# Second layer's down projection of a two-layer decoder by Strassen's scheme of seven products

## The chip, the cores and the metric

The kernel runs on one core of one Trainium2 chip. The metric is the device time of one execution in microseconds, as the median over runs; lower is better. A core has a TensorE (PE in the profile, with PEld for its weight loads), a VectorE (DVE), a ScalarE (ACT), a GpSimd (POOL) and a SyncE (SP). Each engine takes its own instructions in their order. SP, ACT and POOL also issue DMA transfers between the chip's memory and the on-chip memory SBUF.

## The reference

The model is a two-layer decoder over 512 tokens of width 1024, in float32. Each layer ends with a feed-forward block whose hidden width is 2816, and only the second layer's block is touched here:

```python
def conv_ffn(x, ln_g, up_w, conv_w, conv_b, down_w):
    u = causal_dwconv(rms_norm(x, ln_g) @ up_w, conv_w, conv_b)
    gate, up = u[..., :FFN_DIM], u[..., FFN_DIM:]
    return (jax.nn.silu(gate) * up) @ down_w
...
        ff = conv_ffn(x, ffn_ln_g[layer], ffn_up_w[layer], ffn_conv_w[layer],
                      ffn_conv_b[layer], ffn_down_w[layer])
        x = x + ff.astype(x.dtype)
```

The down projection is thus a product of a 512 x 2816 matrix (the hidden values) with a 2816 x 1024 matrix (the weights), and its result is added to the residual stream.

## The kernel before

Every float32 product is made of three products of rounded parts: each operand is split into a high part (a copy to the fp32r type, made by ACT) and a low part (the difference, made by DVE), and PE adds high x high, high x low and low x high into PSUM. One such matrix instruction multiplies a 128 x 128 block into 512 columns.

Weights come as chunks of 128 x 1024 values (512 KB). The list `plan` names them in order of use. `emit_chunk` takes the next one: a DMA issued by SP brings it into one of three raw buffers (`wr_...`), ACT makes `wh_...`, DVE makes `wl_...`, both in rings of three buffers. `chunk(key)` hands out the chunk and sees to it that two more are begun (`AHEAD = 2`).

The second layer's feed-forward (`ffn` with `nnext` None) goes through the 2816 hidden columns in 22 blocks of 128, in two parts of 12 and 10. In the up projection `products` makes, for each block, 24 matrix instructions for the gate (`ps_g`) and 24 for the up side (`ps_u`). `taps` scales a PSUM tile by the row norm on DVE (`uu`, `ug`, L953), applies the three convolution taps (one on ACT, two on DVE, L956), and after SiLU on ACT the block is the product of both sides (L1023). Its high part `hh` is made by ACT (L1024), its low part `hl` by DVE (L1025).

After each part `down_tokens` makes the down projection with hidden values as the stationary operand: for each of two halves of 512 output columns it goes through the part's blocks, and for each block through four blocks of 128 tokens, three matrix instructions each (L992 to L994). The sums are added to `xr`, which holds the residual stream by tokens. In the last part the result is stored in pieces of 128 x 256 by ACT and SP, and the very last products are made in two halves of 256 columns (`end`, L986 to L988) so that the first half's addition and store start earlier.

A scheduler in the kernel's framework turns the program into one queue for each engine; within a queue, an instruction that waits holds up those behind it.

## Time and profile before

| | |
|---|---|
| Median of 3 runs | 1345.41 us (1345.1 to 1346.06) |
| Profiled execution | 1346.14 us |
| ... its span on the chip | 1344.4 us |
| HBM read, written | 131.64 MB, 2.25 MB |
| First down projection of the second layer begins | 1112.3 us after the span's start |
| Second one begins | 1286.4 us |

A page of the profile gives each engine's busy time, the chain of waits that ended last, and groups of instructions as line, engine, operation and "tile written <- tiles read", with the shapes, the count, busy microseconds and the mean in nanoseconds, then the engine's idle time before them and what ended it. A timeline's row begins with the start and the duration in microseconds. PE's matrix instructions are pipelined: each row's duration is longer than the step from one start to the next.

### The profile page before, as it was taken

Reading aid. Unit: us, or ns where it says so; the run is one execution under the profiler, and the core shown is the slowest. Engines: PE = TensorE matmul, PEld = TensorE weight load, DVE = VectorE, ACT = ScalarE, POOL = GpSimd, SP = SyncE. Lnnn points to the kernel's source line nnn. Section 1 sums busy time; section 2 is a strip of 40 time slices with the busy share of each in tenths; the row PEclk is TensorE's granted clock in tenths of the full one; section 3 lists DMA queues with packets and bytes.
Section 4 is the critical chain, followed back from the end, with each engine's and each line's share of the span. In section 5 each row is a group of like instructions: output and inputs, shape, how many; then the busy total and the mean of one; then the engine's idle time right before and its main releaser. Section 6 shows DMA issues by size and latency. Waiting matters only on the chain.

```text
span 1344.4 us, 17006 instructions
## 1 busy us (share of the span) xinstructions
PE 1339.6 (100%) x6468; PEld 1101.9 (82%) x6468; DVE 925.9 (69%) x1554; ACT 645.5 (48%) x1067; POOL 97.8 (7%) x139
## 2 busy tenths in 40 slices
PE   9999999999999999999999999999999999999998
PEld 8878888888888888888888887777888888888887
DVE  7989888889877774367755556778777773367743
ACT  6696554653444442134433556777654442134420
POOL 4230301200110000000002200000100000000000
PEclk9999999999999999999999999999999999999999
DMA  7553533432333333333323423221233333333332
GB/s 205 153 157 95 149 95 114 129 95 70 95 94 98 103 97 94 95 95 101 95 80 111 125 79 94 71 79 49 63 94 94 95 94 94 96 106 96 95 94 79
DMA packets 179826, 135.00 MB, mean 100 GB/s; under 512 B 6492, under 2 KB 163552, under 8 KB 179744
## 3 DMA queue, kind: packets, MB, share of 16 engines
q1 hardware_dynamic: 173872, 120.73, 30.4%
q0 software_dynamic: 4592, 12.08, 3.0%
q8 instruction: 51, 0.84, 0.3%
q10 hardware_dynamic: 1280, 1.10, 0.2%
q14 instruction: 31, 0.25, 0.1%
HBM read 131.64 MB, written 2.25 MB: 100 GB/s over the span
## 4 chain that ended last, share of the span: by engine, by line
PE 98%; DVE 1%; ACT 1%; issue 0%
PE ps_g L205 6%; PE ps_u L206 6%; PE ps_u L204 6%; PE ps_g L206 6%; PE ps_g L204 6%; PE ps_u L205 6%; PE ps_in L204 5%; PE ps_in L206 5%; PE ps_in L205 5%; PE ps_d L206 3%; PE ps_d L205 3%; PE ps_d L204 3%; PE ps_d L992 3%; PE ps_d L994 3%; PE ps_d L993 3%; PE ps_o L205 2%
## 5 line engine op out<-in xcount | busy, mean ns | idle before, releaser
L204 PE MATMUL ps_u<-xgh,wh_u 128*128 128x512 f32 x352 | 137.4, 390 | 0.0
L205 PE MATMUL ps_g<-xgl,wh_g 128*128 128x512 f32 x352 | 137.1, 389 | 0.0
L204 PE MATMUL ps_g<-xgh,wh_g 128*128 128x512 f32 x352 | 137.0, 389 | 0.0
L206 PE MATMUL ps_u<-xgh,wl_u 128*128 128x512 f32 x352 | 137.0, 389 | 0.0
L206 PE MATMUL ps_g<-xgh,wl_g 128*128 128x512 f32 x352 | 137.0, 389 | 0.0
L205 PE MATMUL ps_u<-xgl,wh_u 128*128 128x512 f32 x352 | 136.9, 389 | 0.0
L204 PE MATMUL ps_in<-xgh,wh_in 128*128 128x512 f32 x304 | 122.9, 404 | 0.0
L158 DVE TENSOR_TENSOR wl_d<-wr_d,wh_d 128x1024 fp32r<-128x1024 f32 (+1 forms) x46 | 54.2, 1178 | 96.9 <-ACT wh_d L147 96.7
L206 PE MATMUL ps_in<-xgh,wl_in 128*128 128x512 f32 x304 | 119.7, 394 | 0.0
L205 PE MATMUL ps_in<-xgl,wh_in 128*128 128x512 f32 x304 | 119.1, 392 | 0.0
L147 ACT ACTIVATE wh_d<-wr_d 128x1024 fp32r<-128x1024 f32 (+1 forms) x46 | 47.1, 1024 | 130.6 <-PE ps_d L994 62.4
L953 DVE TENSOR_TENSOR uu<-ps_u,nr_f 128x512 f32<-128x512 f32 x44 | 30.4, 691 | 77.6 <-PE ps_u L206 77.6
L1024 ACT ACTIVATE hh<-vg 128x512 fp32r<-128x512 f32 x44 | 27.8, 632 | 114.9 <-DVE vg L1023 114.9
L205 PEld LDWEIGHTS ps_g<-xgl,wh_g 128*128 128x128 f32 x352 | 66.1, 188 | 14.0 <-DVE xgl L484 0.3
L206 PEld LDWEIGHTS ps_u<-xgh,wl_u 128*128 128x128 f32 x352 | 66.1, 188 | 13.8
L204 PEld LDWEIGHTS ps_g<-xgh,wh_g 128*128 128x128 f32 x352 | 66.1, 188 | 13.7
L206 PEld LDWEIGHTS ps_g<-xgh,wl_g 128*128 128x128 f32 x352 | 66.0, 188 | 13.7
L205 PEld LDWEIGHTS ps_u<-xgl,wh_u 128*128 128x128 f32 x352 | 66.1, 188 | 13.6
L204 PEld LDWEIGHTS ps_u<-xgh,wh_u 128*128 128x128 f32 x352 | 66.1, 188 | 13.5
L147 ACT ACTIVATE wh_g<-wr_g 128x1024 fp32r<-128x1024 f32 x44 | 46.7, 1061 | 50.5 <-PE ps_u L205 31.1
L204 PE MATMUL ps_d<-hh,wh_d 128*128 128x512 f32 x176 | 68.5, 389 | 0.0
L205 PE MATMUL ps_d<-hl,wh_d 128*128 128x512 f32 x176 | 68.5, 389 | 0.0
(374 smaller groups left out, 3198.9 us busy)
## 6 DMA issues: line engine op xcount, KB each, us to landing
wr_g<-in_ffn_up_w_dram SPq DMA_DIRECT2D x44, 512.0 KB, 3.8
wr_u<-in_ffn_up_w_dram SPq DMA_DIRECT2D x44, 512.0 KB, 3.9
wr_d<-in_ffn_down_w_dram SPq DMA_DIRECT2D x42, 512.0 KB, 3.7
wr_in<-in_ssm_in_w_dram SPq DMA_DIRECT2D x40, 512.0 KB, 3.9
m<-cumd POOLq DMA_DIRECT2D x16, 512.0 KB, 4.5
wr_out<-in_ssm_out_w_dram SPq DMA_DIRECT2D x16, 512.0 KB, 3.5
wr_k<-in_kv_w_dram SPq DMA_DIRECT2D x8, 512.0 KB, 3.8
wr_q<-in_q_w_dram SPq DMA_DIRECT2D x8, 512.0 KB, 4.0
```

Of the source, the lines that this page charges most:

```text
L147: return act.activation(self.wh[:, :self.n], self.raw[:, :self.n], AF.Copy)
L158: return eng.tensor_tensor(out=self.wl[:, :self.n], in0=self.raw[:, :self.n], in1=self.wh[:, :self.n].bitcast(F32), op=ALU.subtract)
L204: pe.matmul(ps, wh, xh, start=start, stop=False)
L205: pe.matmul(ps, wh, xl, start=False, stop=False)
L206: return pe.matmul(ps, wl, xh, start=False, stop=stop).ins
L953: dve.tensor_tensor(out=u, in0=ps, in1=r, op=ALU.mult)
L992: pe.matmul(pss[b], hh[k][:, ts], wh[:, k - k0, :], start=k == 0, stop=False)
L993: pe.matmul(pss[b], hh[k][:, ts], wl[:, k - k0, :], start=False, stop=False)
L994: pe.matmul(pss[b], hl[k][:, ts], wh[:, k - k0, :], start=False, stop=k == stop)
L1024: act.activation(h, ga, AF.Copy)
```

## The change

The hidden values are cut in two by tokens (first and last 256) and in two by blocks (even and odd), the weights in two by blocks and in two by output columns. Of the eight block products of a 2 x 2 product the scheme makes seven, of sums of blocks, and adds them up. With A the hidden values (first index token half, second index even or odd blocks) and B the weights (even or odd blocks, column half), the operands are:

| Product | Hidden values | Weights |
|---|---|---|
| 1 | A11 | B11 |
| 2 | A12 | B21 |
| 5 | S1 = A21 - A22 | B11 + B12 |
| 7 | A11 - A21 | B12 + B22 |
| 6 | S2 = S1 - A11 | B11 + B12 + B22 |
| 3 | A12 + S2 | B22 |
| 4 | A22 | B11 + B12 + B22 + B21 |

The blocks are now taken in three parts of 8, 8 and 6, so of 4, 4 and 3 pairs. DVE makes the four sums of hidden values for each pair, and ACT and DVE the high and low parts of seven operands (`operands`). A part's weights B11, B12 and B22 are loaded by SP during its up projection (`ahead`) into the tiles z, x and y; z is two new tiles, x and y lie in `xT`, which is free by then. Ahead of each of these loads POOL copies one column from a hidden block into the tile. B21 alone still comes through the raw buffers. The weights of 5, 6 and 4 are made in z: when a product's weights have been split, POOL issues a DMA that adds the next quarter into z (`plus`). Those of 7 are a sum on DVE. A chunk now covers one product and one or two pairs: 12 or 6 matrix instructions. The products run in the order 1, 2, 5, 7, 6, 3, 4, and within a chunk those with low weights come last. A running sum on DVE (`run_sum`) shares partial results.

```diff
+PARTS_D = (0, 8), (8, 16), (16, 22)
+SEVEN = "1257634"
...
             if l == 1:
-
-                for c in range(2):
-                    for k in range(p0, p1, 2):
-                        plan.append(("d%d_%d_%d" % (l, c, k), *w_cols(ffn_down_w[l], k, 2, c * 512, 512)))
+                for m in SEVEN:
+                    for q0 in range(0, (p1 - p0) // 2, 2):
+                        plan.append(("s%s_%d_%d" % (m, p0, q0), (m, p0, q0, min(2, (p1 - p0) // 2 - q0))))
...
+            def plus(t, p0, q0, nq, j, i):
+                pool.dma_start(view(t, nq), source(p0, q0, nq, j, i), accum_op=ALU.add)
+
+            def ahead(p0, n, behind):
+
+                for k, j, i in ("z", 0, 0), ("x", 0, 1), ("y", 1, 1):
+                    for q0 in range(0, n // 2, 2):
+                        c, nq = q0 // 2, min(2, n // 2 - q0)
+                        pool.tensor_copy(raws[k][c][:, 0:1], behind[:, 0:1])
+                        sync.dma_start(view(raws[k][c], nq), source(p0, q0, nq, j, i))
+
+            def combine(key, m, p0, q0, nq):
+
+                c, n = q0 // 2, nq * 512
+                if m == "2":
+                    t = wrp.tile([P, 1024], F32, tag="raw", name="wr_" + key)
+                    sync.dma_start(view(t, nq), source(p0, q0, nq, 1, 0))
+                else:
+                    t = raws["x" if m == "7" else "y" if m == "3" else "z"][c]
+                    if m == "7":
+                        dve.tensor_tensor(out=t[:, :n], in0=t[:, :n], in1=raws["y"][c][:, :n], op=ALU.add)
...
+                act.activation(wh[:, :n], t[:, :n], AF.Copy)
+                dve.tensor_tensor(out=wl[:, :n], in0=t[:, :n], in1=wh[:, :n].bitcast(F32), op=ALU.subtract)
+                ready.append((key, view(wh, nq), view(wl, nq)))
+                if m in "156":
+                    plus(t, p0, q0, nq, *{"1": (0, 1), "5": (1, 1), "6": (1, 0)}[m])
...
+                    s = fp.tile([P, 4, 256], F32, tag="sums", name="sums%d" % p, bufs=1)
+                    for o, a, b, op in ((0, e[:, 1], h[:, 1], ALU.subtract), (1, s[:, 0], e[:, 0], ALU.subtract),
+                                        (2, e[:, 0], e[:, 1], ALU.subtract), (3, h[:, 0], s[:, 1], ALU.add)):
+                        dve.tensor_tensor(out=s[:, o], in0=a, in1=b, op=op)
+                    parts = [(slice(3, 7), s), (slice(1, 3), h)]
+                for o, v in parts:
+                    act.activation(sh[:, o], v, AF.Copy)
+                    dve.tensor_tensor(out=sl[:, o], in0=v, in1=sh[:, o].bitcast(F32), op=ALU.subtract)
...
+                    for low in range(2):
+                        for b in bs:
+                            for q in qs:
+                                h, w = (t[:, side[m], b * P:(b + 1) * P] for t in sides[q][:2])
+                                if low:
+                                    pe.matmul(pss[b], h, ws[q][1][:, cols], start=False, stop=end and q == qs[-1])
+                                    continue
+                                pe.matmul(pss[b], h, ws[q][0][:, cols], start=first and q == qs[0], stop=False)
+                                pe.matmul(pss[b], w, ws[q][0][:, cols], start=False, stop=False)
...
+                        elif m == "6":
+                            add(r, pss[b])
+                            add(to(b, 512), r, ALU.subtract)
+                            add(r, seven[b])
+                            add(to(2 + b, 512), r, ALU.subtract)
+                            add(to(2 + b, 0), r)
```

The orders of the queues up to the second layer's first block are the same as before. At three places they show what moved.

SP, before, in the up projection of the second layer around blocks 5 and 6 (`wr_g1_5` is the raw buffer for block 5's gate weights):

```order
L139 DMA wr_g1_5_8982<-in_ffn_up_w_dram 128x8x128
L139 DMA wr_u1_5_9020<-in_ffn_up_w_dram 128x8x128
L139 DMA wr_g1_6_9062<-in_ffn_up_w_dram 128x8x128
L139 DMA wr_u1_6_9100<-in_ffn_up_w_dram 128x8x128
L139 DMA wr_g1_7_9142<-in_ffn_up_w_dram 128x8x128
```

and the same place now (`wz0`, `wz1` are z, `xT` is x and y):

```order
L140 DMA wr_g1_5_9007<-in_ffn_up_w_dram 128x8x128
L140 DMA wr_u1_5_9045<-in_ffn_up_w_dram 128x8x128
L994 DMA wz0_8586<-in_ffn_down_w_dram 128x2x512
L994 DMA wz1_8587<-in_ffn_down_w_dram 128x2x512
L994 DMA xT_85<-in_ffn_down_w_dram 128x2x512 x4
L140 DMA wr_g1_6_9087<-in_ffn_up_w_dram 128x8x128
```

The first part's six loads of down weights now stand between block 5's and block 6's up weights.

DVE, before, from the last block's up side (`uu1_21`) into the second down projection (`wl_d1_0_16` is the low part of a chunk of down weights):

```order
L953 TENSOR_TENSOR uu1_21_10787<-ps_u1_21_10762,nr_f1_8671 128x512
L158 TENSOR_TENSOR wl_d1_0_16_10805<-wr_d1_0_16_10802,wh_d1_0_16_10804 128x1024
L956 SCALAR_TENSOR_TENSOR vu1_21_10788<-uu1_21_10787,cf1_105,vu1_21_10788 128x511
L956 SCALAR_TENSOR_TENSOR vu1_21_10788<-uu1_21_10787,cf1_105,vu1_21_10788 128x510
L1023 TENSOR_TENSOR vg1_21_10750<-vg1_21_10750,vu1_21_10788 128x512
L1025 TENSOR_TENSOR hl1_21_10794<-vg1_21_10750,hh1_21_10793 128x512
L158 TENSOR_TENSOR wl_d1_0_18_10835<-wr_d1_0_18_10832,wh_d1_0_18_10834 128x1024
```

and now (`wl_s2_16_0` is the low part of product 2's weights for the first two pairs of the part that begins at block 16, `wl_s2_16_2` that of its third pair, `ps_s1_16_0` the sum of product 1 for the first 128 tokens, `sl20` the low operands of the pair 20, 21):

```order
L957 TENSOR_TENSOR uu1_21_11046<-ps_u1_21_11021,nr_f1_8674 128x512
L1009 TENSOR_TENSOR wl_s2_16_0_11067<-wr_s2_16_0_11064,wh_s2_16_0_11066 128x1024
L960 SCALAR_TENSOR_TENSOR vu1_21_11047<-uu1_21_11046,cf1_105,vu1_21_11047 128x511
L1009 TENSOR_TENSOR wl_s2_16_2_11085<-wr_s2_16_2_11082,wh_s2_16_2_11084 128x512
L960 SCALAR_TENSOR_TENSOR vu1_21_11047<-uu1_21_11046,cf1_105,vu1_21_11047 128x510
L1059 TENSOR_TENSOR xr_8585<-xr_8585,ps_s1_16_0_11062 128x512
L1132 TENSOR_TENSOR vg1_21_11010<-vg1_21_11010,vu1_21_11047 128x512
L1059 TENSOR_TENSOR xr_8585<-xr_8585,ps_s1_16_1_11063 128x512
L1035 TENSOR_TENSOR sums21_11053<-vg1_20_10931,vg1_21_11010 128x256
L1039 TENSOR_TENSOR sl20_10976<-vg1_21_11010,sh20_10975 128x512
L1035 TENSOR_TENSOR sums21_11053<-sums21_11053,vg1_20_10931 128x256
L1009 TENSOR_TENSOR wl_s5_16_0_11101<-wz0_8586,wh_s5_16_0_11100 128x1024
```

The split of product 2's second chunk and the additions for product 1 now stand ahead of the last pair's low operands.

DVE, now, around product 6 of the last part:

```order
L1009 TENSOR_TENSOR wl_s6_16_0_11171<-wz0_8586,wh_s6_16_0_11170 128x1024
L1009 TENSOR_TENSOR wl_s6_16_2_11188<-wz1_8587,wh_s6_16_2_11187 128x512
L1009 TENSOR_TENSOR wl_s3_16_0_11201<-xT_85,wh_s3_16_0_11200 128x1024
L1009 TENSOR_TENSOR wl_s3_16_2_11217<-xT_85,wh_s3_16_2_11216 128x512
L1059 TENSOR_TENSOR run_sum_8588<-run_sum_8588,ps_s6_16_0_11198 128x512
L1059 TENSOR_TENSOR run_sum_8588<-run_sum_8588,ps_s6_16_1_11199 128x512
L1059 TENSOR_TENSOR xr_8585<-xr_8585,run_sum_8588 128x512 x2
L1059 TENSOR_TENSOR run_sum_8588<-run_sum_8588,ps_s7_16_0_11168 128x512
L1059 TENSOR_TENSOR run_sum_8588<-run_sum_8588,ps_s7_16_1_11169 128x512
L1059 TENSOR_TENSOR xr_8585<-xr_8585,run_sum_8588 128x512 x4
L1009 TENSOR_TENSOR wl_s4_16_0_11243<-wz0_8586,wh_s4_16_0_11242 128x1024
```

Ten additions stand between product 3's and product 4's weights.

131 lines of the change are left out of this document (91 added, 40 removed).

## The prediction

> **What bounds the kernel now.** I read the page's engine shares first, then its chain of waits, then the stages of the second layer's feed-forward, then single instructions.
>
> ```profile
> span 1344.4 us, 17006 instructions
> PE 1339.6 (100%) x6468; PEld 1101.9 (82%) x6468; DVE 925.9 (69%) x1554; ACT 645.5 (48%) x1067; POOL 97.8 (7%) x139
> PE 98%; DVE 1%; ACT 1%; issue 0%
> ```
>
> TensorE is busy for the whole span and makes up 98% of the chain: no wait is left to remove, and only fewer products, or cheaper ones, shorten it. The view of busy time by stage, cut at the first down projection, the up projection of blocks 12 to 21, the second down projection and the tail, says how much room the other engines have:
>
> ```profile
> 1112.30:1177.60 65.30, 65.30 (x289) 54.06 (x289) 22.67 (x24) 14.07 (x14) 0.00 (x0) 1.00 0.32 96
> 1177.60:1286.40 108.80, 108.80 (x481) 90.09 (x480) 76.82 (x96) 47.76 (x59) 0.00 (x0) 1.00 0.33 98
> 1286.40:1341.00 54.60, 54.60 (x247) 45.30 (x245) 19.47 (x29) 9.82 (x10) 0.00 (x0) 1.00 0.25 78
> ```
>
> Columns: length, then busy us of PE, PEld, DVE, ACT and POOL, granted clock, DMA share, GB/s. PE fills each stage; DVE is at 71% in the up projection (76.82 of 108.80) and at 35% in the down projections. The price of a product is its pitch, not the 0.39 us of its row, since products overlap:
>
> ```profile
> 1135.46 0.39 PE L992 MATMUL ps_d<-wh_d,hh 128*128 128x512 f32 x1
> 1135.68 0.39 PE L993 MATMUL ps_d<-wl_d,hh 128*128 128x512 f32 x1
> L992 PE MATMUL ps_d<-wh_d,hh 128*128 128x512 f32 x174 | 67.7, 389 | 0.0
> L986 PE MATMUL end<-wh_d,hh x4: 278/283/283, 1339.5 to 1340.5; 128*128 128x256 f32 x4
> 1339.81 0.28 PE L986 MATMUL end<-wh_d,hh 128*128 128x256 f32 x1
> 1340.77 0.28 PE L988 MATMUL end<-wh_d,hl 128*128 128x256 f32 x1
> ```
>
> The first down projection has 288 products of 512 columns in 65.30 us: 0.2267 us each (1135.46 to 1135.68 shows one step). The eight steps from 1339.81 to 1340.77 give 0.12 us for one of 256 columns.
>
> **The products removed (term 1).** Before: 2 column halves x 22 blocks x 4 token blocks x 3 = 528, of which the last 6 are cut into 12 half-width ones: 522 full (three lines of 174) and 12 half. After: 7 sums x 11 pairs x 2 token blocks x 3 = 462, the last 3 cut into 6: 459 full and 6 half. Saved: 63 x 0.2267 + 6 x 0.12 = 15.0 us. The new order inside a product (low weights last) loads one stationary tile per product as before, so it changes no pitch.
>
> **DVE's new work (term 2).** These rows price it:
>
> ```profile
> L158 DVE TENSOR_TENSOR wl_d<-wr_d,wh_d 128x1024 fp32r<-128x1024 f32 x42 | 51.5, 1226 | 96.9 <-ACT wh_d L147 96.7
> L1025 DVE TENSOR_TENSOR hl<-vg,hh 128x512 fp32r<-128x512 f32 x11 | 7.6, 693 | 7.7 <-ACT hh L1024 7.7
> 1140.83 1.23 DVE L158 TENSOR_TENSOR wl_d<-wr_d,wh_d 128x1024 fp32r<-128x1024 f32 x1 [4.21 <-ACT wh_d L147]
> 1141.97 1.28 DVE L999 TENSOR_TENSOR xr<-ps_d,xr 128x512 f32<-128x512 f32 x2
> 1283.19 1.53 DVE L956 SCALAR_TENSOR_TENSOR vg<-ug,cf,vg 128x511 f32<-128x511 f32 x2
> 1336.94 0.76 DVE L1005 TENSOR_TENSOR xr<-ps_d,xr 128x256 f32<-128x256 f32 x2 [0.67 <-PE ps_d L994]
> 1341.09 0.42 DVE L1005 TENSOR_TENSOR xr<-end,xr 128x256 f32<-128x256 f32 x1 [0.29 <-PE end L988]
> L147 ACT ACTIVATE wh_d<-wr_d 128x1024 fp32r<-128x1024 f32 x42 | 44.6, 1062 | 124.8 <-PE ps_d L994 62.4 <-PE ps_d L205 49.2 <-PE ps_u L205 6.6
> ```
>
> Queued back to back, independent DVE instructions overlap by some 0.08 us: the split that starts at 1140.83 is followed at 1141.97, so 1.14 us for 1024 columns; the pair of 0.69 takes 1.28, so 0.60 for 512; the pair of 0.42 takes 0.76, so 0.34 for 256. The two taps (L956) take 1.53.
>
> In the up projection two blocks take PE 4 x 24 x 0.2267 = 21.8 us and DVE now 71% of that, 15.4. Two low parts of 512 go (1.2); four sums of 256, and low parts of 256, 512 and 1024 come (3.4), and per part two sums of 1024 for product 7 (0.6 per two blocks): 18.2 us, 84%. Still under PE; cost nothing.
>
> In the down projection of a part of eight blocks PE has 168 x 0.2267 = 38.1 us. DVE has: the rest of the last block (PSUM times norm 0.60, taps 1.53, gate times up 0.60, three sums 1.0, low parts 0.60 and 1.14: 5.5), twelve splits (13.7), 22 additions (13.2; ten of them after product 6), two splits for the next blocks (2.3): 34.7. It fits, but with one thin place. Product 2's second chunk needs the second half of the last block's operands after 36 products, 8.2 us. Ahead of them DVE has, counting in queue order, 0.60, 0.3 of waiting for ACT's copy, 1.14, 1.53, the second split of product 2 (it stands before the gate product) 1.14, 0.60, 0.60, 0.34, 0.60, 0.34, and then 0.69: 7.9 us. Margin 0.3; I take 0.
>
> In the last part PE has 123 x 0.2267 + 6 x 0.12 = 28.6 us, and DVE 5.5, six splits of 1024 and six of 512 (10.4), 22 additions (13.2) and two of 256 (0.7): 29.8 us. So there DVE ends last. It also waits some 1.4 us: 0.3 at the start, 0.3 for product 3's buffer, 0.5 for the end of product 6, the rest in handoffs. It ends about 31.3 us after the last up product, 2.7 past PE. Before, DVE's last addition ended at 1341.51, 55.1 us after 1286.4, where PE needed 234 x 0.2267 + 12 x 0.12 = 54.5: 0.6 past. Cost: 2.1 us. If DVE were slower or its queue less full of ready work, this is the term that grows; if PE were held up elsewhere, it shrinks.
>
> **The accumulating loads (term 3).** After product 1's weights are split, z takes another quarter of the matrix by a DMA from POOL that adds into SBUF, and so after 5 and 6. No row shows such a transfer. The nearest:
>
> ```profile
> wr_d<-in_ffn_down_w_dram SPq DMA_DIRECT2D x42, 512.0 KB, 3.7
> m<-cumd POOLq DMA_DIRECT2D x16, 512.0 KB, 4.5
> wr_d<-in_ffn_down_w_dram SPq DMA_DIRECT2D x4, 256.0 KB, 3.1
> DMA to landing us min/median/max: 3.8/4.5/7.9
> out_dram<-xr SPq DMA_DIRECT2D x8, 128.0 KB, 1.9
> out_dram<-xr ACTq DMA_DIRECT2D x8, 128.0 KB, 2.6
> ```
>
> The half-size load is 0.6 us shorter, so 512 KB move in about 1.2 us. From below: 4.5, as POOL's plain load of this size (the fourth line is its spread). From above: three times that, 13.5. Reading the target too doubles the moving part only: 4.5 + 1.2 = 5.7, which I take as nearest to the row. Its deadline: the split of the sum before must end, the load land, and ACT copy 1.06 us before PE starts the next use. In the last part product 5's split ends at 8.5 us (0.1 of handoff, 0.60, 0.3 of waiting, 1.14, 0.75, 0.60, 0.75, 0.60, 0.60, 0.60, 0.34, 0.60, 0.34, 1.23 in queue order), product 6 starts at 72 x 0.2267 = 16.3: 6.7 us for the load. Ten more rows and its own (0.34, 0.60, 0.60, 1.14, 0.60, 1.14, 0.60, 2.40, 1.23) bring product 6's split to 17.1; product 4 starts at 108 x 0.2267 = 24.5: 6.3 us. In the parts of eight blocks these are 11 us or more, 9.7 once the first load itself delays the second split. So 5.7 is covered, by 0.6 at the worst place. With a spread that reaches 7.9 I add 0.5 us. What is late otherwise: ACT's copy for product 6 waits, behind it on ACT the copies for product 3, and PE for both; two such waits per part. On POOL only other accumulations stand behind.
>
> **What is moved (term 4).** Six loads of a part (3 MB) stand on SP between two up-weight loads, for the first part behind block 5's. POOL's six one-column copies ahead of them have by then long been done (block 2). A load on SP has this slack:
>
> ```profile
> 1228.90 0.37 SPq L139 DMA_DIRECT2D wr_g<-in_ffn_up_w_dram  x1
> 1231.99 1.06 ACT L147 ACTIVATE wh_g<-wr_g 128x1024 fp32r<-128x1024 f32 x1 [0.94 <-PE ps_u L205]
> 1237.43 1.07 ACT L147 ACTIVATE wh_u<-wr_u 128x1024 fp32r<-128x1024 f32 x1 [0.28 <-PE ps_g L205]
> 1242.87 1.06 ACT L147 ACTIVATE wh_g<-wr_g 128x1024 fp32r<-128x1024 f32 x1 [0.94 <-PE ps_u L205]
> ```
>
> With three raw buffers the load issued at 1228.90 is the one split at 1242.87, 14.0 us later, and PE reads it two chunks of 24 products (10.9 us) later, since the plan runs two chunks ahead. The next load is issued one chunk (5.4 us) after, behind six of 1.2 us; even if all seven ran one after another at 3.7 (25.9 us), it would land 24 us after its issue and cost PE under 2. I take 0. On ACT two stores of the last part stand ahead of product 6's copy and wait for product 2's additions at 12 us; that copy is not due before 15. The very last store moves from SP to ACT: by the two rows above 0 to 0.7 us; I take 0.3.
>
> **Sum.** -15.0 + 2.1 + 0.5 + 0.3 = -12.1 us. The profiled execution took 1346.14 with a span of 1344.4: 1334.0, with a span of 1332.3. The median of the runs shown is 0.7 lower: 1345.41 - 12.1 = 1333.3 us.
>
> **The rivals.** A: the accumulating load takes twice the plain one, 9.0 us. Both deadlines of the last part are missed, by 2.3 and 2.7, less the 0.5 allowed: 1333.3 + 4.5 = 1337.8. For it: an add must read both operands; against it: only a third of the 4.5 scales with size. (The Trainium skill, Collectives: The Full Stack, section "The bandwidth ceiling", says that a transfer with an add ran at about half the rate of a copy, 32.35 against 62.28 GB/s, because it reads two sources. By that rule on the whole 4.5 us this rival holds, on the moving part alone the 5.7 above; no run shows it yet.)
>
> B: DVE instructions on one accumulator don't overlap, since each addition to the output tile or to the running sum touches what the one before wrote. Then about 40 instructions in the last part cost 0.08 more, 3.2, and the thin places in the two earlier parts (margin 0.3 against ten such steps, and the ten additions ahead of product 4's split) some 1.9 each: 1333.3 + 7.0 = 1340.3. For it: dependent taps take 1.53, no overlap; against it: most neighbours in the new queue are independent.
>
> C, slower: the accumulating loads are far slower than any load here. Each microsecond of their time A costs 2 past 6.5 us in the last part and 4 more past 9.7 in the other two: -12.6 + 2(A - 6.5) + 4(A - 9.7) is zero at A = 10.7. At 13.5, three times the row, it is +16.6: 1362.0. Against it: the longest POOL load of this size took 7.9.
>
> D: nothing but the products counts, because loads and DVE stay hidden: 1345.4 - 15.0 = 1330.4. Against it the 29.8 to 28.6 above.
>
> **Chances.** The forecast 0.46, A 0.18, B 0.13, C 0.13, D 0.05; 0.05 is left for the meeting of A and C near zero and for what I don't see. The forecast alone lies within 1331 to 1335; the range takes in A, B and D: 1330 to 1342. A change under 0.2% (2.7 us) can't be told from none. Faster: the forecast, A, B and D, 0.82; slower: C and 0.02 of the rest, 0.15; same 0.03.
>
> **What would show it.** Step 1: three lines of products that total 459 + 6 at a pitch of 0.2267. Step 2: DVE busy over 90% from the last up product to the end, PE idle about 2 us there and under 0.5 at the two earlier parts. Step 3: the adding loads land within 6.3 us and ACT's copies for products 6 and 4 wait for them without PE waiting. Step 4: no wait of PE in the up projection. The prediction is wrong if PE idles before product 6 or 4 behind those copies, or before product 2's second chunk behind DVE.

## The result and the profile after

| | Before | After |
|---|---|---|
| Median of 4 runs each, same chip | 1345.31 us (1345.1 to 1346.06) | 1333.62 us (1333.47 to 1334.21) |
| Ratio, 95% interval | | 0.9913 (0.9896 to 0.993) |
| Profiled execution, its span | 1346.14, 1344.4 us | 1333.75, 1332.1 us |

The change made the kernel 11.7 us faster; 1333.3 was predicted, in a range of 1330 to 1342. The page of the kernel after:

```profile
PE 1325.3 (99%) x6399; PEld 1088.0 (82%) x6399; DVE 1001.3 (75%) x1678; ACT 671.6 (50%) x1104; POOL 121.8 (9%) x175
PE 94%; DVE 4%; ACT 1%; DMA 1%; issue 0%; SPq 0%; POOL 0%; DVEq 0%; ACTq 0%
```

TensorE lost 14.3 us of busy time (1339.6 to 1325.3) and the span lost 12.3. The chain, 98% TensorE before, now runs 4% through VectorE. How the stages share this, the view of busy time by stage says (length; busy us of PE, PEld, DVE, ACT and POOL; granted clock; DMA share; GB/s). The stages are the down projection of the first part, the up and down projection of the second, and the down projection of the third:

```profile
1067.83:1105.91 38.08, 38.08 (x170) 31.53 (x168) 33.20 (x43) 18.69 (x20) 4.83 (x4) 1.00 0.51 96
1105.91:1192.95 87.04, 87.04 (x386) 72.07 (x384) 70.81 (x96) 38.27 (x50) 3.56 (x8) 1.00 0.48 140
1192.95:1231.03 38.08, 38.08 (x170) 31.53 (x168) 33.18 (x43) 18.68 (x20) 4.83 (x4) 1.00 0.50 95
...
1296.31:1326.72 30.41, 30.24 (x130) 23.34 (x128) 28.01 (x42) 13.60 (x18) 4.19 (x4) 1.00 0.48 96
```

The parts of eight blocks take 38.08 us each, which is 168 products at 0.2267 us and nothing else; the up projection of eight takes 87.04, which is 384 products. So in these stages TensorE waits nowhere up to 1296.31, where the last part begins. That part would take 28.6 us at the same pitch and takes 30.41, with VectorE busy for 28.01 of it (92%), and 5.38 us pass behind it.

For a comparison that does without the run's beginning, take the first product of the second layer's feed-forward, before and after. The timeline of the kernel before:

```profile
977.08 0.39 PE L204 MATMUL ps_g<-xgh,wh_g 128*128 128x512 f32 x1
```

and of the kernel after:

```profile
976.09 0.39 PE L208 MATMUL ps_g<-xgh,wh_g 128*128 128x512 f32 x1
```

The work ahead of it is the same, so the 0.99 us is between two executions and not the change's (in the other kernels below, whose work up to here is the same too, it stands between 976.29 and 977.53). From there to the end of the span: 367.32 us before, 356.01 after, 11.31 less. (The medians say 11.7.)

How VectorE comes into the last part and ends it, in its timeline after (start, duration, instruction, in brackets the idle time ahead of it and what ended it):

```profile
1279.41 1.23 DVE L1005 TENSOR_TENSOR xT<-xT 128x1024 f32<-128x1024 f32 x1 [1.91 <-DMA xT<-in_ffn_down_w_dram]
...
1296.51 0.69 DVE L957 TENSOR_TENSOR uu<-ps_u,nr_f 128x512 f32<-128x512 f32 x1 [0.17 <-PE ps_u L210]
1298.05 1.23 DVE L1009 TENSOR_TENSOR wl_s<-wr_s,wh_s 128x1024 fp32r<-128x1024 f32 x1 [0.85 <-ACT wh_s L1008]
...
1304.19 1.22 DVE L1009 TENSOR_TENSOR wl_s<-wz,wh_s 128x1024 fp32r<-128x1024 f32 x1
...
1313.49 1.23 DVE L1009 TENSOR_TENSOR wl_s<-wz,wh_s 128x1024 fp32r<-128x1024 f32 x1 [0.60 <-ACT wh_s L1008]
1315.25 0.69 DVE L1009 TENSOR_TENSOR wl_s<-wz,wh_s 128x512 fp32r<-128x512 f32 x1 [0.53 <-ACT wh_s L1008]
1316.20 1.83 DVE L1009 TENSOR_TENSOR wl_s<-xT,wh_s 128x1024 fp32r<-128x1024 f32 x2 [0.25 <-ACT wh_s L1008]
...
1321.54 2.49 DVE L1059 TENSOR_TENSOR xr<-xr,run_sum 128x512 f32<-128x512 f32 x4
1323.94 1.82 DVE L1009 TENSOR_TENSOR wl_s<-wz,wh_s 128x1024 fp32r<-128x1024 f32 x2
1325.68 2.47 DVE L1059 TENSOR_TENSOR xr<-xr,ps_s 128x512 f32<-128x512 f32 x4
1328.26 0.75 DVE L1059 TENSOR_TENSOR xr<-xr,end 128x256 f32<-128x256 f32 x2
```

VectorE ends at 1329.01, 32.70 us after the last up product. It waited 2.4 us there (the five brackets from 1296.51 on) and 0.1 at the end, so 30.2 us are work. From 1316.20 on its queue has no gap of note: TensorE's last products, those with product 4's low weights, wait for the splits at 1323.94, and the four additions from 1325.68 are still running when they are done. Behind VectorE's end 3.09 us of storing follow (before: 1344.4 - 1341.51 = 2.89).

The first row stands in the up projection ahead of that part: VectorE waits 1.91 us for x and y, which it adds up for product 7, and no room is left behind it to make that up (one gap of 0.29 us until 1296.51). The chain that ended last passes through this load, and from there through VectorE's queue to TensorE's wait at 1303.99:

```profile
1270.98 8.31 DMA xT<-in_ffn_down_w_dram
```

How much of the wait reaches the last part, other kernels' executions say, whose queue on VectorE in this up projection is the same. In the kernels below called "four additions later", "no adding loads" and "six additions left out" it was 1.12, 1.48 and 1.75 us, and VectorE began product 2's first split (here at 1298.05) 1.06, 1.31 and 1.57 us after the last up product; here, with 1.91, 1.74. So a wait of 1.12 us is absorbed (1.06 is also the start in parts of six that VectorE enters with time to spare), and here 0.7 us come through.

The bookkeeping from the first up product on: products 15.0 less; VectorE's end 32.70 - 28.6 = 4.1 us past what TensorE needs, where it was 0.6 before, 3.5 more; storing 0.2 more: -11.3.

The loads that add into z, on the page (512 KB each, median us to landing):

```profile
wz<-in_ffn_down_w_dram POOLq DMA_DIRECT2D x15, 512.0 KB, 6.0
```

and in the view of their line (POOL's time for an issue in ns, min/median/max; then who waited, us and times):

```profile
L986 POOL DMA_DIRECT2D wz<-in_ffn_down_w_dram x18: 889/1190/1517, 1060.2 to 1316.2; - x18
  ACT wh_s L1008: 15.2, 6
```

They take 6.0 us, and ACT's copies of z waited for them six times, 15.2 us in all. The last part's, in the timeline of POOL and ACT (a row of POOL's holds two loads, issued one after the other; those for product 4 start at 1315.02):

```profile
1305.94 2.12 POOL L986 DMA_DIRECT2D wz<-in_ffn_down_w_dram  x2 [10.23 <-DVE sums L1035]
...
1312.40 1.06 ACT L1008 ACTIVATE wh_s<-wz 128x1024 fp32r<-128x1024 f32 x1 [4.55 <-DMA wz<-in_ffn_down_w_dram]
1314.58 0.63 ACT L1008 ACTIVATE wh_s<-wz 128x512 fp32r<-128x512 f32 x1 [1.12 <-DMA wz<-in_ffn_down_w_dram]
...
1320.89 1.06 ACT L1008 ACTIVATE wh_s<-wz 128x1024 fp32r<-128x1024 f32 x1 [4.21 <-DMA wz<-in_ffn_down_w_dram]
```

The first load of product 6 is issued at 1305.94 and copied from 1312.40, 6.5 us later; the second, behind it on POOL, only from 1314.58. TensorE's timeline shows a little of that, and one wait for VectorE ahead of it (a row's start is set against the start of the row ahead plus 0.2267 us for each of its products):

```profile
1303.12 0.73 PE L1055 MATMUL ps_s<-wh_s,sh 128*128 128x512 f32 x2
1303.99 0.74 PE L1056 MATMUL ps_s<-wh_s,sl 128*128 128x512 f32 x2
...
1312.87 0.61 PE L1053 MATMUL ps_s<-wl_s,sh 128*128 128x512 f32 x2
1313.51 0.50 PE L1055 MATMUL ps_s<-wh_s,sh 128*128 128x512 f32 x1
1313.85 0.40 PE L1056 MATMUL ps_s<-wh_s,sl 128*128 128x512 f32 x1
```

Two products take 0.45 us. So product 2's second chunk goes on 0.42 us late at 1303.99 (for the low part `sl` of the last block's hidden values, which VectorE, late by those 0.7 us, finished at 1303.93), product 6 begins 0.19 late at 1313.51, with a step of 0.34 instead of 0.23 behind it, and product 4 begins 0.16 late at 1322.00.

### The profile page after: what moved, and what is told of

It reads as the page before. It is cut to its first block, busy times and chain, and to the rows that moved or that the text cites. A ratio compares the mean times of both kernels' runs of the same rounds, so it can differ in the third digit from the quotient of the medians.

```text
span 1332.1 us, 17130 instructions
## 1 busy us (share of the span) xinstructions
PE 1325.3 (99%) x6399; PEld 1088.0 (82%) x6399; DVE 1001.3 (75%) x1678; ACT 671.6 (50%) x1104; POOL 121.8 (9%) x175
## 4 chain that ended last, share of the span: by engine, by line
PE 94%; DVE 4%; ACT 1%; DMA 1%; issue 0%; SPq 0%; POOL 0%; DVEq 0%; ACTq 0%
PE ps_g L209 5%; PE ps_u L208 5%; PE ps_g L210 5%; PE ps_g L208 5%; PE ps_u L209 5%; PE ps_u L210 5%; PE ps_in L208 5%; PE ps_in L210 5%; PE ps_in L209 5%; PE ps_d L210 3%; PE ps_d L209 3%; PE ps_d L208 3%; PE ps_s L1056 2%; PE ps_s L1055 2%; PE ps_s L1053 2%; PE ps_o L209 2%
## 5 line engine op out<-in xcount | busy, mean ns | idle before, releaser
L208 PEld LDWEIGHTS ps_u<-xgh,wh_u 128*128 128x128 f32 x352 | 66.0, 188 | 13.5
L1127 ACT ACTIVATE vg<-vg 128x512 f32<-128x512 f32 x44 | 27.8, 633 | 84.0 <-DVE vg L960 84.0
L148 ACT ACTIVATE wh_u<-wr_u 128x1024 fp32r<-128x1024 f32 x44 | 46.8, 1063 | 43.8 <-PE ps_g L209 35.4
L210 PE MATMUL ps_d<-hh,wl_d 128*128 128x512 f32 x176 | 68.5, 389 | 0.0
L960 DVE SCALAR_TENSOR_TENSOR vu<-uu,cf,vu 128x511 f32<-128x511 f32 x88 | 65.8, 748 | 3.1 <-ACT vu L958 1.7
```

The costliest lines, as they stand in the source:

```text
L148: return act.activation(self.wh[:, :self.n], self.raw[:, :self.n], AF.Copy)
L208: pe.matmul(ps, wh, xh, start=start, stop=False)
L210: return pe.matmul(ps, wl, xh, start=False, stop=stop).ins
L960: dve.scalar_tensor_tensor(out=v[:, s:], in0=u[:, :T - s], scalar=col(2 - s), in1=v[:, s:], op0=ALU.mult, op1=ALU.add)
L1127: act.activation(ga, ga, AF.Silu)
```

## The experiments

The theory to test: of the 15.0 us of products about 3.5 are given back, all in the last part, because VectorE's queue there is longer than TensorE's and no later work takes that up; waits behind the adding loads make part of it. The main rival is that the adding loads alone are the price.

All kernels in one table, each compared with runs of the kernel before beside its own; "rest" is the time from the first up product to the end of the span, in its profiled execution, as above (before: 367.32). The intervals of the ratios are some 2 us either way, so a difference of one or two us is not settled by an interval. It rests on single executions that repeat one another: VectorE's end in the last part comes 31.72 and 31.73 us after the last up product in the two kernels without additions into z, and 39.14 in each of the three with parts of 6 and 8 whose additions all stay on VectorE. Storing took 3.09 us in the changed kernel's execution and 2.84 to 2.94 in all others, so some 0.2 us of each difference is storing.

| Kernel | Median, us | Ratio (95%) | Rest, us | Against the change |
|---|---|---|---|---|
| the change | 1333.62 | 0.9913 (0.9896 to 0.993) | 356.01 | |
| no adding loads | 1333.41 | 0.9906 (0.9891 to 0.992) | 354.84 | -1.2 |
| plain loads in their place | 1333.18 | 0.9905 (0.9892 to 0.9919) | 354.83 | -1.2 |
| adding loads twice | 1364.95 | 1.0147 (1.013 to 1.0164) | 386.66 | +30.7 |
| six additions left out | 1332.22 | 0.9897 (0.9882 to 0.9912) | 354.04 | -2.0 |
| parts 6, 8, 8 | 1332.64 | 0.9899 (0.9883 to 0.9916) | 354.17 | -1.8 |
| parts 8, 6, 8 | 1332.70 | 0.9897 (0.9881 to 0.9914) | 354.22 | -1.8 |
| four additions later | 1333.99 | 0.991 (0.9895 to 0.9925) | 355.36 | -0.7 |
| parts 6, 8, 8, four additions later | 1332.71 | 0.99 (0.9885 to 0.9915) | 354.57 | -1.4 |
| parts 6, 8, 8, four additions on POOL | 1335.02 | 0.9922 (0.9909 to 0.9936) | 356.93 | +0.9 |
| low products among the others | 1336.40 | 0.9931 (0.9919 to 0.9944) | 359.51 | +3.5 |
| first loads of a part late | 1343.26 | 0.9979 (0.997 to 0.9988) | 365.18 | +9.2 |

### What the adding loads cost

```diff
-                if m in "156":
+                if False:
                     plus(t, p0, q0, nq, *{"1": (0, 1), "5": (1, 1), "6": (1, 0)}[m])
```

> Leaves out the 18 loads that add a quarter of the matrix into z, so products 5, 6 and 4 use z's first quarter; all copies, splits, products and additions stay. Theory (VectorE's queue sets the end of the last part: 30.0 us of work and 2.4 us of waits after the last up product, 1.4 us of these behind copies of z that wait for such a load): the waits go in part, TensorE's 0.9 us of lateness at products 6 and 4 too; 0.8 us faster than the changed kernel (0.3 to 1.4), about 1332.8. Rival 1 (the loads are the main price of the change, as in rival A): 3 us faster or more, at or under 1330.6. Rival 2 (the loads are hidden altogether): within 0.2 us of 1333.6.

Measured: 1.2 us less by the profile, 0.9 by the ratios. In VectorE's timeline the three waits behind ACT's copies at 1313 to 1316 are gone; its last row, and one of TensorE's (the first product of the last part is at 1297.33):

```profile
1325.26 1.43 PE L1053 MATMUL ps_s<-wl_s,sh 128*128 128x512 f32 x5 [0.28 <-DVE wl_s L1009]
1328.30 0.75 DVE L1059 TENSOR_TENSOR xr<-xr,end 128x256 f32<-128x256 f32 x2
```

VectorE ends 31.72 us after the last up product, against 32.70: with the loads its queue ended 1.0 us later. And without them TensorE still waits for VectorE's split at the end. Rival 1 falls (1.2 and not 3). Against rival 2 (hidden altogether) stands VectorE's end, here and in the next kernel, and not the medians: 1333.41 is only 0.2 under 1333.62.

The 1.0 us needs two things, though: the adding loads, and a VectorE that is late. Here VectorE caught up at product 6 and waited 0.37 us for TensorE before that product's additions, which began 20.64 us after the last up product (in the changed kernel 21.63). In "four additions later" the adding loads are in place, the wait for x and y was shorter (1.12 us), and the same additions began at 20.65. In the parts of six of "parts 6, 8, 8" and "parts 8, 6, 8", where VectorE came on time as well, they began at 20.54 and 20.58, and VectorE waited for no adding load at product 6. The timeline of VectorE in parts 6, 8, 8, where the part of six begins at 1047.56:

```profile
1063.52 1.82 DVE L1009 TENSOR_TENSOR wl_s<-wz,wh_s 128x1024 fp32r<-128x1024 f32 x2
...
1068.10 1.29 DVE L1059 TENSOR_TENSOR run_sum<-run_sum,ps_s 128x512 f32<-128x512 f32 x2 [0.37 <-PE ps_s L1053]
```

So the 1.0 us is the price of both together: the loads of x and y make VectorE late, its late split delays the issue of the next adding load, and VectorE then waits for that. No kernel was run that changes only the wait for x and y.

What the addition itself costs was measured with loads that overwrite z:

```diff
-                pool.dma_start(view(t, nq), source(p0, q0, nq, j, i), accum_op=ALU.add)
+                pool.dma_start(view(t, nq), source(p0, q0, nq, j, i))
```

> The loads into z are issued on POOL as before but overwrite z instead of adding to it, so products 5, 6 and 4 use the last quarter alone. It measures the price of the addition by itself. The prediction's step (an addition doubles the moving part only: 1.2 us on top of the plain load): landing in 4.8 us instead of 6.0 by the median of 512 KB, POOL's issue 0.55 us instead of 1.2, and with the loads inside their deadlines the whole about 0.8 us faster than the changed kernel, like the kernel without these loads. Rival (the addition costs nothing, the 6.0 is POOL's queue and the traffic of the weights): landing and time as in the changed kernel. Rival (half the rate on the whole load): 3.0 us instead of 6.0.

The page's row of these loads:

```profile
wz<-in_ffn_down_w_dram POOLq DMA_DIRECT2D x15, 512.0 KB, 4.1
```

and the view of their line:

```profile
L986 POOL DMA_DIRECT2D wz<-in_ffn_down_w_dram x18: 567/722/786, 1060.8 to 1315.2; - x18
```

A plain load of the same 512 KB by the same queue lands in 4.1 us, the adding one in 6.0: the addition costs 1.9 us, and POOL's issue is 0.5 longer (0.72 to 1.19). That is 1.5 times, neither "the moving part only" (1.2 more) nor twice. (The Trainium skill, Collectives: The Full Stack, section "The bandwidth ceiling: the fold count and why AG ≠ RS ≠ AR", has a collective that adds at about half the rate of one that copies; by that rule on the whole load one would estimate 8.2 us here, and the row says 6.0.) The time is that of the kernel without these loads, so in a last part that VectorE enters late a load of 4 us is hidden altogether and one of 6 costs 1.0 to 1.2.

How steep it gets beyond, with each addition made twice:

```diff
-                    plus(t, p0, q0, nq, *{"1": (0, 1), "5": (1, 1), "6": (1, 0)}[m])
+                    for _ in range(2):
+                        plus(t, p0, q0, nq, *{"1": (0, 1), "5": (1, 1), "6": (1, 0)}[m])
```

> Issues each adding load twice, so z takes the quarter twice over and the weights of products 5, 6 and 4 are others than the reference's. If the second waits for the first, an addition takes A = 12 us in place of 6.0, and the line of the prediction's rival C (2 us per us of A past 6.5 in the last part, 4 more past 9.7 in the other two) gives 11 + 9 = 20 us slower than the changed kernel, about 1354. If the two run side by side, A is 6.0 and one issue on POOL of 1.2, about 7.2: 1.5 us slower, 1335. A theory in which the loads have room to spare everywhere: no change in either case.

The second load did wait for the first, and it cost 30.7 us instead of 20. By parts: 47.27, 47.71 and, to VectorE's end, 44.32 us, where the change has 38.08, 38.08 and 32.70. The last part's 11.6 more is what the prediction's line gives (2 x 5.5 = 11). The two parts of eight lose 9.2 and 9.6, twice what the line gives (4.6). In the view of the loads' line, who waited for them:

```profile
  POOL wz L986: 52.0, 15
```

POOL itself waits for the first of two loads before it issues the second, with the other chunk's loads queued behind, so those come later than 12 us. And in TensorE's timeline the products behind a wait are slow:

```profile
1243.60 0.50 PE L1056 MATMUL ps_s<-wh_s,sh 128*128 128x512 f32 x1 [2.67 <-ACT wh_s L1008]
...
1244.88 0.63 PE L1057 MATMUL ps_s<-wh_s,sl 128*128 128x512 f32 x1
```

From the row at 1244.88 to the next, at 1245.30, it is 0.42 us, not 0.23. The window of these 3 us has the reason, a granted clock of 0.50:

```profile
1244.88:1247.86 2.98, 2.98 (x8) 2.30 (x7) 0.65 (x1) 1.74 (x2) 0.00 (x0) 0.50 0.11 19
```

So a wait of 2.7 us cost more than its length here. Shorter ones did so too, though not all of them; the last section has the list.

### VectorE's queue in the last part

```diff
-                            add(to(b, 512), r, ALU.subtract)
+                            if not last:
+                                add(to(b, 512), r, ALU.subtract)
                             add(r, seven[b])
-                            add(to(2 + b, 512), r, ALU.subtract)
-                            add(to(2 + b, 0), r)
+                            if not last:
+                                add(to(2 + b, 512), r, ALU.subtract)
+                                add(to(2 + b, 0), r)
```

> Leaves out, in the last part only, the six additions of product 6 that go into the output tile (three per token block), so three quarters of the output lack that product in the last part. Theory (VectorE's queue sets the end): 6 x 0.60 = 3.6 us of queued work go, VectorE then ends as soon as the last product does (0.6 us after, in place of 1.9), and TensorE keeps its 1.8 us of lateness: 1.3 us faster than the changed kernel, 1332.3 (1331.8 to 1332.8). Rival 1 (TensorE held by the loads sets the end, VectorE has room): within 0.3 us of 1333.6. Rival 2 (additions on one accumulator don't overlap and VectorE is the whole price): 3 us faster or more, 1330.6.

Measured: 2.0 us less by the profile, more than the 1.3 expected. Not all of it is the additions': product 6's additions began 21.17 us after the last up product instead of 21.63, ahead of everything that was left out, in part because the wait for x and y was 1.75 us and not 1.91. TensorE's lateness was not kept either: its last product starts 29.66 us after the last up product instead of 30.29, since the splits stood behind those additions. A row of VectorE's:

```profile
1322.83 1.83 DVE L1009 TENSOR_TENSOR wl_s<-wz,wh_s 128x1024 fp32r<-128x1024 f32 x2 [1.83 <-ACT wh_s L1008]
```

Now VectorE idles ahead of product 4's split (1.83 us, for the copy that waits for its load): with a shorter queue the load ends last. Of 3.6 us taken away some 1.4 arrive, besides the 0.5 from ahead of them and 0.2 of storing; the loads are the next bound. Rival 1 and rival 2 fall.

Then the same relief without leaving anything out, by the sizes of the parts:

```diff
-PARTS_D = (0, 8), (8, 16), (16, 22)
+PARTS_D = (0, 6), (6, 14), (14, 22)
```

> Only the sizes of the parts change: 6, 8 and 8 blocks instead of 8, 8 and 6. Theory (VectorE's queue is too long only for a part of six, and only in the last part does nothing come after to take that up): in a last part of eight VectorE has 33 us of work and some 2.4 us of waits under TensorE's 37.9, so the end comes 0.6 us behind the last product as before the change, in place of 1.9, and TensorE's 1.8 us of lateness go down to under 1; in the first part of six up to 1.5 us of lateness come back at products 2, 6 and 4, VectorE's backlog of 3 us is worked off in the up projection. Sum: 1.5 us faster than the changed kernel, 1332.1 (1331 to 1333.5). Rival (the loads' deadlines are the price and they move with the part of six): 1333.6 or slower. If the backlog of the first part is not worked off in the up projection: 1335 or slower.

Measured: 1.8 us less, and where it was expected. The last part, now of eight blocks, has no wait of TensorE (38.11 us from 1289.71 to the end of its last product), and VectorE's last addition ends 1.0 us after that product, where the change has 2.3. VectorE has more room in two ways: its queue is short for eight blocks, and the sums for product 7 begin 39 us ahead of the part's first product instead of 17, so that a wait for x and y is made up. This kernel's timeline of TensorE and VectorE:

```profile
1075.39 1.20 PE L1053 MATMUL ps_s<-wl_s,sh 128*128 128x512 f32 x4 [0.68 <-DVE wl_s L1009]
...
1322.66 2.35 DVE L1009 TENSOR_TENSOR wl_s<-wz,wh_s 128x1024 fp32r<-128x1024 f32 x2
...
1327.70 0.28 PE L1053 MATMUL end<-wl_s,sh 128*128 128x256 f32 x1
1328.10 0.75 DVE L1059 TENSOR_TENSOR xr<-xr,end 128x256 f32<-128x256 f32 x2
```

The part of six, now first, holds TensorE up at one place above all: 0.68 us of idling in the first row, 0.85 late by the pitch, where product 4's split stands behind product 6's ten additions; smaller steps make it some 1.3 in all. Its backlog is worked off in the up projection. With the part of six in the middle it is the same:

```diff
-PARTS_D = (0, 8), (8, 16), (16, 22)
+PARTS_D = (0, 8), (8, 14), (14, 22)
```

> Parts of 8, 6 and 8 blocks. Theory (it matters only that the part of six isn't the last one): like the parts of 6, 8 and 8, which took 1.8 us less than the changed kernel by their ratios to the kernel before: within 0.4 us of that. Rival (the first part had slack that the middle one hasn't): 0.5 us slower than 6, 8 and 8 or more.

Measured: 354.22 us for the rest, against 354.17.

Two attempts at the 0.85 us that are left. First, four of product 6's additions were moved behind product 3, so that the split comes ahead of them:

```diff
                             add(r, seven[b])
+                        elif m == "3":
                             add(to(2 + b, 512), r, ALU.subtract)
                             add(to(2 + b, 0), r)
-                        elif m == "3":
                             add(to(b, 512), pss[b])
...
-                        stores((2, 3) if m == "6" else (0, 1), 0 if m == "2" else 512)
+                        if m == "3":
+                            stores((2, 3), 512)
+                        if m != "6":
+                            stores((0, 1), 0 if m == "2" else 512)
```

The stores of what these additions finish move with them. Of the two kernels one has the parts of 6, 8 and 8 besides, the other the change's own.

> Parts of 6, 8 and 8 blocks, and four of product 6's ten additions (the second running sum into the lower half of the output) moved behind product 3, so that the splits for product 4 stand ahead of them in VectorE's queue. Theory (TensorE's lateness of 0.85 us at product 4 in the part of six is VectorE's split standing behind ten additions): 4 x 0.60 = 2.4 us less stands ahead of the split, the lateness goes: 0.7 us faster than 6, 8 and 8 alone (0.4 to 1). Rival (the split waits for its load or for ACT's copy): no change from 6, 8 and 8.

> The same four additions moved behind product 3, with the changed kernel's own parts of 8, 8 and 6. Theory (there VectorE's whole queue sets the end, and this only changes its order): TensorE's 0.45 us at product 4 go, VectorE's end stays: 0.2 us faster than the changed kernel (0 to 0.5). Rival (the order of the queue, not its length, is the price): 1 us faster or more, as far as the parts of 6, 8 and 8 came.

With the change's own parts the time is 0.7 us less by the profile and 0.4 by the ratios, but that isn't shown to be the order's: 0.25 us of it is storing, and VectorE was 0.98 us ahead when product 6's additions began, before anything that was moved in the last part, above all since it had waited 1.12 us for x and y and not 1.91. Of these 0.98 us 0.43 were left at its end; the split for product 4, now early, waited 0.46 us for ACT's copy of the loaded z. TensorE's steps at product 4 stayed, at 0.1 us each. With the parts of 6, 8 and 8 the new order brought nothing. The wait at the split is gone and another stands in its place, at the next up weights (TensorE's timeline):

```profile
1077.69 0.50 PE L210 MATMUL ps_g<-xgh,wl_g 128*128 128x512 f32 x1 [1.31 <-DVE wl_g L159]
```

So there the length of VectorE's queue was the limit, and its order only chose what is late; the theory of that expectation fell.

Second, four of the ten additions were given to POOL, with the second running sum (`r7`) in a tile of its own:

```diff
...
-                            add(to(b, 512), r, ALU.subtract)
-                            add(r, seven[b])
-                            add(to(2 + b, 512), r, ALU.subtract)
-                            add(to(2 + b, 0), r)
+                            pool.tensor_tensor(out=to(b, 512), in0=to(b, 512), in1=r, op=ALU.subtract)
+                            dve.tensor_tensor(out=r7, in0=r, in1=seven[b], op=ALU.add)
+                            pool.tensor_tensor(out=to(2 + b, 512), in0=to(2 + b, 512), in1=r7, op=ALU.subtract)
+                            add(to(2 + b, 0), r7)
```

> Parts of 6, 8 and 8 blocks, and four of product 6's ten additions (those between two SBUF tiles that go into the second column half) on POOL, with the second running sum in a tile of its own. Theory: VectorE's queue was short of room only in the part of six, where TensorE was late by 1.2 us in all with 0.85 of it at one split; 4 x 0.60 = 2.4 us of that queue go, the lateness goes to 0.4 or less, and the end of the last part stays, since VectorE waits there already: 0.5 us faster than with the parts of 6, 8 and 8 alone (0 to 0.9). POOL's additions at 1.5 us each (its rows of that size) take 6 us a part and are in nobody's way. Rival (POOL's additions slow VectorE or hold the stores at the end): 0.5 us slower or more.

The rival was right: 2.8 us slower than with the parts alone. VectorE and POOL in the last part's timeline:

```profile
1317.77 2.55 POOL L1102 TENSOR_TENSOR xr<-xr,run_sum 128x512 f32<-128x512 f32 x2 [4.23 <-DVE run_sum L1059]
1318.19 1.28 DVE L1103 TENSOR_TENSOR r<-run_sum,ps_s 128x512 f32<-128x512 f32 x2
1319.39 3.18 DVE L1059 TENSOR_TENSOR xr<-xr,r 128x512 f32<-128x512 f32 x2
1320.29 3.43 POOL L1104 TENSOR_TENSOR xr<-xr,r 128x512 f32<-128x512 f32 x2
1322.49 3.44 DVE L1009 TENSOR_TENSOR wl_s<-wz,wh_s 128x1024 fp32r<-128x1024 f32 x2
```

While POOL adds, two of VectorE's additions take 3.18 us instead of 1.28, and two splits 3.44 instead of 2.35; POOL's own go from 2.55 to 3.43 for two. (The Trainium skill, SBUF — State Buffer, section "SBUF: two separate sides", says that a VectorE instruction with two inputs in SBUF and a GpSimd one that reads SBUF exclude each other, whichever starts first. The rows agree nearly: from 1319.39 to 1325.93 VectorE had 3.6 us of work and POOL 3.5 by their undisturbed rows, 7.1 one after the other, and they took 6.5.) The additions at 1318.19, which read PSUM, are not slowed.

### The order inside a product, and the loads during the up projection

The place of the products of low weights, undone:

```diff
-                    for low in range(2):
-                        for b in bs:
-                            for q in qs:
...
+                    for b in bs:
+                        for q in qs:
+                            h, w = (t[:, side[m], b * P:(b + 1) * P] for t in sides[q][:2])
+                            pe.matmul(pss[b], h, ws[q][0][:, cols], start=first and q == qs[0], stop=False)
+                            pe.matmul(pss[b], w, ws[q][0][:, cols], start=False, stop=False)
+                            pe.matmul(pss[b], h, ws[q][1][:, cols], start=False, stop=end and q == qs[-1])
```

> Undoes one part of the change: the product with a pair's low weights stands right behind the other two again, not behind all eight of its chunk. Theory: the pitch stays at 0.2267 us, but a chunk's low weights are due 1.4 us earlier (third product of the chunk instead of the ninth: 6 x 0.2267). Where VectorE's split ends last (the last part, products 2, 5, 6 and 4) TensorE then waits up to 1.4 us more each time, part of which is inside VectorE's own lateness: 1 us slower than the changed kernel (0.3 to 3), about 1334.6. Rival (the order inside a product does nothing): within 0.2 us of the changed kernel.

Measured: 3.5 us slower by the profile, 2.4 by the ratios: the direction was right, the size at the far end. 3.0 of it lie in the last part. The pitch is the same until shortly before the end; two waits carry the loss, and a slow clock behind the second:

```profile
1316.48 0.50 PE L1051 MATMUL ps_s<-wh_s,sh 128*128 128x512 f32 x1 [1.65 <-ACT wh_s L1008]
1327.23 0.50 PE L1053 MATMUL ps_s<-wl_s,sh 128*128 128x512 f32 x1 [1.81 <-DVE wl_s L1009]
```

The second is product 4's split behind product 6's additions. From 1 us after it the granted clock was 0.53 (1328.20 to 1331.32), and a step took up to 0.43 us: the seven products of 512 columns from 1328.27 to 1331.12 took 2.85 us, where 1.59 would do at the usual pitch. That is 1.3 of the 3.0 us. This part of the change, costed at nothing in the prediction, is worth some 3 us here: it makes the low weights due 1.4 us later in a chunk of two pairs, and 0.45 in a chunk of one, and without it a wait of 1.81 us was followed by half the clock.

The loads of a part moved from behind its third block to behind its last but one:

```diff
-                        if p == p0 + 2:
+                        if p == p1 - 2:
                             ahead(p0, p1 - p0, ga)
```

> The six loads of a part are issued behind the part's last block but one, instead of behind its third. z is then issued some 5 us before ACT's copy of it and 13 us before TensorE's first product with it. Theory (these loads have slack, and the up projection hides them wherever they stand): z lands 4 to 7 us after its issue, ACT is held up to 2 us in a stage where it is about half busy, TensorE not at all: within 0.5 us of the changed kernel. Rival (six loads between two weight loads of the up projection hold it): three times 1 to 3 us, 1337 or more, with TensorE waiting for copies of the up weights.

It cost 9.2 us in this execution; the ten runs lie far apart, from 1338.87 to 1345.22, so the size is uncertain. Neither theory was right: the rival's time (1337 or more) was met, but the loss isn't in the up projection. The expectation's working had a mistake: block 20 is ready one block later than assumed, and z is issued 6.3 us ahead of the first product with it, not 13. The up projection lost nothing, as the theory said; the down projections of the three parts lost 1.7, 4.8 and (to VectorE's end) 2.9. In the second a wait of 2.38 us is followed by a granted clock of 0.50 (1208.5 to 1211.0). POOL's adding loads, ACT and TensorE in the last part, whose first product is at 1303.55:

```profile
1303.64 2.11 POOL L986 DMA_DIRECT2D wz<-in_ffn_down_w_dram  x2 [5.62 <-DVE wl_s L1009]
1310.03 1.06 ACT L1008 ACTIVATE wh_s<-wz 128x1024 fp32r<-128x1024 f32 x1 [3.79 <-DMA wz<-in_ffn_down_w_dram]
1311.00 0.61 ACT L1038 ACTIVATE sh<-vg 128x512 fp32r<-128x512 f32 x1
1311.66 0.96 PE L1055 MATMUL ps_s<-wh_s,sh 128*128 128x512 f32 x3 [1.15 <-ACT sh L1038]
```

The first adding load now starts after the first product instead of 5.8 us ahead of it; ACT's copy for product 5 waits for it, and behind that copy stands the high part of the last block's hidden values, which product 2 needs. The early place of these loads is what lets product 1's adding loads run in the up projection.

## Why the prediction was right

**The products (term 1).** Right to 0.1 us: the two parts of eight take 38.08 us each where 38.1 stood, at the same pitch. No new wait of TensorE stands between up and down projections.

**VectorE in the last part (term 2).** Right in kind, too small in size: 2.1 us in the sum. Its work was 30.2 us (29.8 predicted), its waits 2.5 (1.4 predicted). Without the adding loads VectorE ends 31.72 us after the last up product, so 31.72 - 28.6 - 0.6 = 2.5 us are its own. That the queue itself is the price, the parts of 6, 8 and 8 and the six additions left out show. The prediction's count was good where VectorE came on time: in the parts of six of 6, 8, 8 and 8, 6, 8 product 5's first split ended 8.54 us after the last up product, where it had 8.5.

**The adding loads (term 3).** The load was put at 5.7 us and measured 6.0; the bound from above, 13.5, was far off. The statement that it is covered "by 0.6 at the worst place" failed: here that split ended 9.1 us after 1296.31 (at 1305.41), 0.6 later than counted, as VectorE came late, POOL's issue began 0.5 later still, and two chunks' loads go one behind the other on POOL. The cost was 1.0 us at VectorE's end, against the 0.5 allowed for the spread, and it is shared with term 4. By its own test (wrong if TensorE idles before product 6 or 4 behind those copies, or before product 2's second chunk behind VectorE) the step was wrong by little: 0.2 us at product 6, as much at product 4, and at product 2's second chunk, the thin place, 0.4 in the last part and none in the parts of eight. These, a second such wait at product 4 and the slower steps behind each make up most of the 1.8 us between 28.6 and 30.41.

**What is moved (term 4).** Taken at 0, and right only for TensorE in the up projection: 87.04 us for 384 products. The term looked at the weights that stand behind the six loads and not at who reads the loads themselves. In the last part's up projection VectorE waited 1.91 us for x and y, whose load took 8.31 us (on the page 7.0 by the median of 512 KB, where a load of up weights takes 3.8), and 0.7 us of that came into the last part. The last store on ACT: storing took 0.2 us longer than before, and 2.84 to 3.09 in all the runs here, so 0 to 0.2 of the 0.3.

**The sum.** -15.0 + 2.5 (VectorE's queue) + 1.0 (the loads, moved and adding) + 0.2 (storing) = -11.3 from the first up product on, where -12.1 was predicted. The predicted span, 1332.3, was met to 0.2 only because the profiled execution started its feed-forward 0.99 us sooner; the median is 0.3 above the predicted one.

**The rivals.** A: the loads took 6.0 and not 9.0. B: the additions keep their step of 0.60 (the four at 1321.54 take 2.49), because neighbours in the queue go to different parts of a tile, by token block or column half. Its premise stands: where an instruction reads what the one ahead wrote, nothing overlapped (the gate product at 1256.56 is followed by the first sum 0.73 us later and that by the second after 0.45, against 0.60 and 0.34 for independent ones). C: its mechanism is real and steeper than its line in the parts of eight (30.7 us for a load twice as long), but its condition isn't met. D, nothing but the products, falls to the last part's 3.5 us; VectorE's queue alone accounts for 2.5 of them.

The best kernels here that leave nothing out have the change with its part of six first or in the middle: 1332.64 us, ratio 0.9899 (0.9883 to 0.9916), and 1332.70, both 1.8 us under the change by their profiles. The intervals overlap with the change's.

## What to carry to other kernels

In this kernel a product less on a full TensorE was worth its pitch as long as the other engines' queues were shorter than its own in every stage; what was given back was given back in the last stage, where nothing follows that could take up a backlog. So put the smallest part, the one with the most side work per product, anywhere but last. A load that stands between two splits should be priced with its queue: the issue, the other chunk's load ahead of it, and what stands behind the copy that waits for it. And a load that is moved is to be priced at its reader too: one that makes an engine wait shortly before the stage in which that engine has no room carries the wait into it.

## What the runs showed of the hardware

- While POOL added between SBUF tiles, VectorE's additions between SBUF tiles took 2.5 times as long (3.18 us for 1.28), and those that read PSUM did not (1.28).
- A load that adds into SBUF took 1.5 times a plain one (6.0 to 4.1 us for 512 KB), with 1.19 us of POOL's time to issue instead of 0.72.
- After some waits TensorE was granted half its clock (0.50), beginning within 2 us of its going on and for 2.5 us or more, and products of 512 columns came at 0.42 to 0.43 us. It followed waits of 2.67 and 2.06 us ("adding loads twice", at 1243.60 and 1338.89), 2.38 ("first loads of a part late", 1206.53) and 1.81 ("low products among the others", 1327.23), and not those of 1.99 ("adding loads twice", 1109.33) and 1.65 ("low products among the others", 1316.48), so the length alone doesn't decide it here. (The Trainium skill, TensorE: Matmul & The Clock Gate, section "What's actually happening", speaks of half rate after an idle window of about 3.4 us; here shorter waits were enough.) Waits of 0.2 us cost one step of 0.34 instead of 0.23 on top, with the clock at 1.00.
